# A two-layer transformer block on one core: the durations that its list scheduler assumes for TensorE and GpSimd are changed

## The chip, the cores and the metric

The kernel runs on one core of a Trainium2 chip, in one launch. A core has five instruction queues that run side by side and meet only at semaphores: TensorE (PE: matmuls and transposes), VectorE (DVE), ScalarE (ACT), GpSimd (POOL) and SyncE (SP), which here issues the DMAs. Each works through its instructions strictly in the order in which the program was written out for it. The metric is the device time of one execution in microseconds; the median of three is given. The profile comes from one more execution.

## The reference

A stack of two layers works on 256 tokens `x` and 256 context tokens `ctx`, both 1024 wide, in fp32. Each layer is a feed-forward block, a token mix (neighbourhood attention over the 256 tokens and the context with 8 heads of 64, beside a pooling mix over 4 groups of 128 channels), and a second feed-forward block. Every block is normed before and after, and modulated by nine vectors that come from a condition through a 1024 x 9216 matrix per layer.

```python
def sandwich_ffn(x, w_gate_up, w_down, g_pre, g_post, shift, scale, gate):
    h = modulate(rms_norm(x, g_pre), shift, scale)
    return x + 0.5 * gate * rms_norm(swiglu(h, w_gate_up, w_down), g_post)

for l in range(DEPTH):
    ...
    x = sandwich_ffn(x, w_ffn_gate_up[l, 0], w_ffn_down[l, 0], g[0], g[1], mx[0], mx[1], mx[2])
    ctx = sandwich_ffn(ctx, w_ffn_gate_up[l, 0], w_ffn_down[l, 0], g[0], g[1], mc[0], mc[1], mc[2])
    hx = modulate(rms_norm(x, g[2]), mx[3], mx[4])
    hc = modulate(rms_norm(ctx, g[2]), mc[3], mc[4])
    out_x, out_c = token_mix(hx, hc, w_in[l], w_out[l], na_rpb[l], w_pool[l], pool_scale[l], not last)
    x = x + mx[5] * rms_norm(out_x, g[3])
    x = sandwich_ffn(x, w_ffn_gate_up[l, 1], w_ffn_down[l, 1], g[4], g[5], mx[6], mx[7], mx[8])
    if not last:
        ctx = ctx + mc[5] * rms_norm(out_c, g[3])
        ctx = sandwich_ffn(ctx, w_ffn_gate_up[l, 1], w_ffn_down[l, 1], g[4], g[5], mc[6], mc[7], mc[8])
return x
```

## The kernel before

**Arithmetic.** Every fp32 operand of a large matmul is split into a high part in the matmul format `fp32r` and a low part, the rest. A product is three matmuls (`mm3`: high by high, high by low, low by high). Splitting is an ACT copy into the high half and a DVE subtraction into the low half (`split`, and the same in `Stream.prep` for weights). A weight tile of 1024 columns so costs one ACT and one DVE instruction of 1024 elements per partition; the tiles are called `w_big`.

**Stages.** The program runs `ffn(0, 0)`, `token_mix(0)`, `ffn(0, 1)`, `ffn(1, 0)`, `token_mix(1)`, `ffn(1, 1)`. A feed-forward block walks over 22 groups of 128 hidden columns: gate (`pg`) and up (`pu`), 24 matmuls each, the SiLU product, then the down matmuls into `pd`. Its hidden columns go in parts (`F_GROUPS`), the down matmuls of each part adding to `y_big`. In `ffn(1, 0)` the gate and up matmuls of a group are replaced by seven quarter products (`gate_up_seven`, tiles `p_ps`), whose sums of weights GpSimd forms (`prep_seven`, tiles `s_wk`). `close` ends a block per token tile: squares on ACT, `power` on GpSimd (a sum and a power of -0.5, tiles `rs`), scaling, and the transposes that make the next block's input.

**Attention.** `token_mix` runs the eight heads as chains (`head`): scores `pS` and `pC` on PE, maxima on DVE, exponentials on ACT, normalising, transposes `pp`, splitting, and the products `po`. Between them stand blocks of 24 column matmuls for the keys (`pk`), queries (`pq`) and the pooling input (`pu`) of the next pair of heads. `pooled` forms the window sums on GpSimd (`dd`), and `roped` turns keys and queries with one product on GpSimd and the rest on DVE.

**Filler.** The modulation vectors that later blocks need are accumulated on DVE (`acc`, from `wm` tiles of the modulation matrix) and added up on GpSimd (`part`), spread over the feed-forward blocks by `fill`.

**What sets the order.** Nothing is issued while these functions run. Each call is recorded (`Recorder.record`) as an operation with a price (`Recorder.price`), its dependencies by overlap of what it reads and writes, and its place in the record (`rank`). `Recorder.order` then plays a list schedule: every engine has a clock; of all operations whose inputs are done, the one that can start earliest by these clocks is taken, a lower `rank` first where two tie, with small head starts (`haste`) for the ends of blocks and for heads, and a `margin` for a few. It also decides from these times when a buffer place comes free (16 places for `big`, 2 for raw weights, 10 for `wk`, 8 PSUM banks, 24 for small statistics), which tile gets which place, and in which order SP issues the DMAs. `Recorder.issue` writes the operations out in that order. The prices do nothing else: no value, size or dependency depends on them. All operations so carry the line of `issue`, L387, in the profile, and are told apart by their tiles.

Of the kernel before, what the change touches and what calls it, by code (L numbers as in the profile page):

```python
# [12 lines left out]
F32R = mybir.dt.float32r  # L13
# [171 lines left out]
class Recorder:  # L185
# [30 lines left out]
    @staticmethod  # L216
    def price(engine, method, outs, ins, kw):
        size = max(int(np.prod(v.shape[1:])) for v in outs + ins if isinstance(v, View)) if engine != "sync" else 0
        far = any(isinstance(v, View) and v.buf.tag == "ps" for v in ins)
        pointers = sum(1 for v in ins if isinstance(v, View) and int(np.prod(v.shape[1:])) == 1 and size > 1)  # L220
        if engine == "tensor":
            n = int(np.prod(outs[0].shape[1:]))
            if method == "transpose":
                return 0.107
            return 0.003 + n / 2400.0 if ins[0].dtype == F32R else 0.19
        if engine == "scalar":
            extra = 0.093 * (min(pointers, 1) + (1 if "accum_out" in kw else 0))
            return (0.052 if far else 0.094) + size / 1200.0 + extra
        if engine == "vector":
            rate = 0.52 if method in ("tensor_scalar", "tensor_copy") and not far else 1.042  # L230
            return 0.068 + rate * size / 1000.0 + 0.061 * min(pointers, 2)
        if engine == "gpsimd":
            if method == "memset":
                return 0.03 + size / 1200.0
            if kw.get("op") == ALU.pow:
                return 0.464
            return 0.155 + 2.09 * size / 1000.0
        return 0.45

    def record(self, engine, method, args, kw):  # L240
# [1255 lines left out]
```

## Time and profile before

| | us |
|---|---|
| median of 3 executions | 1657.24 |
| their lowest and highest | 1656.57, 1659.04 |
| the profiled execution | 1658.03 |
| its span, first to last instruction | 1656.0 |
| mean granted TensorE clock | 0.996 of full |

The span is what the views of the profile divide; the other 2.0 us of the profiled execution lie around it. PE is TensorE's matmuls, PEld its weight loads beside them. A matmul's busy time reaches until its result is out, so successive matmuls overlap in the record. "Idle before" is the time that an engine stood still ahead of an instruction, with the engine or transfer that released it. The windows view gives busy times in stretches of the span; the chain is the work that ended last, followed back from the end. Busy times in tenths over 40 equal slices of the span show the parts: the first slice is the start, slices 11 to 14 hold the attention of layer 0, and 33 to 36 that of layer 1:

```
PE   6999999999999899999999999999999999899998
DVE  7985766546689779867776488677788778875554
ACT  7522322225566663222222264534444567774442
POOL 1022011101131311110211036363463122210000
```

### The profile page before, as it was taken

The page shows a single profiled execution, that of the slowest core. Times are in us where ns is not written, and L with a number is a line of the kernel's source. Part 1 is how long each engine was busy: PE and PEld are TensorE (multiplying, and loading weights), DVE is VectorE, ACT ScalarE, POOL GpSimd, SP SyncE. Part 2 cuts the span into 40 slices and gives each one's busy share as a digit, 9 for nine tenths or more (in the row PEclk, how much of TensorE's full clock was granted, in tenths as well). Part 3 has the DMA queues.
Part 4 walks back from the last instruction along what each step waited for, and adds up shares of the span by engine and source line. Part 5 has one row for each costly group of instructions (what it writes and reads, how often), then busy time and mean ns, then how long its engine had stood idle before and what let it go on. Part 6 is the DMA issues. An engine that isn't in the chain of part 4 may idle for free.

```text
span 1656.0 us, 23501 instructions
## 1 busy us (share of the span) xinstructions
PE 1613.0 (97%) x9074; PEld 1390.3 (84%) x9074; DVE 1212.7 (73%) x1662; ACT 736.6 (44%) x1292; POOL 356.9 (22%) x348
## 2 busy tenths in 40 slices
PE   6999999999999899999999999999999999899998
PEld 4988888888878689888888879999989888778997
DVE  7985766546689779867776488677788778875554
ACT  7522322225566663222222264534444567774442
POOL 1022011101131311110211036363463122210000
PEclk9999999999999999999999999999999999999999
DMA  9466556532221436666698412233233421355551
GB/s 376 185 230 243 209 194 225 175 118 83 86 78 65 157 108 223 235 204 230 211 351 300 159 52 96 83 103 127 77 116 114 144 90 70 132 200 199 196 200 55
DMA packets 98958, 269.09 MB, mean 162 GB/s; under 512 B 9424, under 2 KB 39328, under 8 KB 87072
## 3 DMA queue, kind: packets, MB, share of 16 engines
q1 hardware_dynamic: 98848, 267.60, 45.5%
q8 instruction: 71, 1.16, 0.3%
q14 instruction: 39, 0.32, 0.1%
HBM read 251.80 MB, written 1.09 MB: 153 GB/s over the span
## 4 chain that ended last, share of the span: by engine, by line
PE 84%; DVE 6%; ACT 5%; POOL 2%; issue 2%; DMA 1%; SPq 0%; POOLq 0%; DVEq 0%; ACTq 0%
PE pd_ps L387 26%; PE pu_ps L387 19%; PE pg_ps L387 19%; PE p_ps L387 11%; PE pv_ps L387 2%; ACT n_wk L387 2%; PE pk_ps L387 2%; POOL rs_st L387 2%; DVE w_big L387 1%; PE pq_ps L387 1%; DMA w_big<-in_wmod_dram 1%; PE pt_ps L387 1%; ACT sx_wk L387 1%; PE po_ps L387 1%; ACT w_big L387 1%
## 5 line engine op out<-in xcount | busy, mean ns | idle before, releaser
L387 DVE TENSOR_TENSOR w_big<-raw_raw,w_big 128x1024 fp32r<-128x1024 f32 x293 | 369.8, 1277 | 122.5 <-ACT w_big L387 122.2
L387 PE MATMUL pd_ps<-w_big,g_big 128*128 128x512 f32 x1848 | 430.7, 393 | 0.0
L387 PEld LDWEIGHTS pd_ps<-w_big,g_big 128*128 128x128 f32 x1848 | 345.7, 188 | 77.7 <-ACT grows L387 0.2
L387 ACT ACTIVATE w_big<-raw_raw 128x1024 fp32r<-128x1024 f32 x293 | 302.8, 1054 | 228.9 <-DMA raw_raw<-in_wgu_dram 94.6
L387 PE MATMUL pu_ps<-h_big,w_big 128*128 128x512 f32 (+1 forms) x1944 | 366.4, 341 | 0.0
L387 PEld LDWEIGHTS pu_ps<-h_big,w_big 128*128 128x128 f32 x1944 | 303.7, 188 | 42.5
L387 PE MATMUL pg_ps<-h_big,w_big 128*128 128x512 f32 (+1 forms) x1752 | 330.3, 342 | 1.4 <-ACT h_big L387 1.4
L387 PEld LDWEIGHTS pg_ps<-h_big,w_big 128*128 128x128 f32 x1752 | 275.6, 189 | 41.3 <-ACT h_big L387 1.8
L387 DVE SCALAR_TENSOR_TENSOR acc_wk<-wm_wk,csil,acc_wk 128x1024 f32<-128x1024 f32 x196 | 244.2, 1285 | 81.5 <-DMA wm_wk<-in_wmod_dram 81.2
L387 POOL TENSOR_TENSOR part_wk<-part_wk 128x512 f32<-128x512 f32 (+2 forms) x84 | 87.7, 1045 | 496.1 <-DMA part_wk<-acc_wk 418.5
L387 ACT ACTIVATE g_big<-tt_wk 128x512 fp32r<-128x512 f32 (+1 forms) x84 | 49.2, 586 | 275.6 <-DVE tt_wk L387 258.4
L387 POOL TENSOR_SCALAR rs_st<-sq_st 128x1 f32<-128x1 f32 x24 | 7.5, 312 | 448.8 <-ACT n_wk L387 448.7
L387 POOL TENSOR_TENSOR s_wk<-raw_raw 128x512 f32<-128x512 f32 x38 | 64.1, 1695 | 126.3 <-DMA raw_raw<-in_wgu_dram 120.5
L387 PE MATMUL p_ps<-h_big,w_big 128*128 128x256 f32 x684 | 86.8, 281 | 0.0
L387 PEld LDWEIGHTS p_ps<-h_big,w_big 128*128 128x128 f32 x684 | 83.5, 189 | 0.3
L387 PE MATMUL p_ps<-ht_big,w_big 128*128 128x256 f32 x684 | 82.9, 279 | 0.0
L387 PEld LDWEIGHTS p_ps<-ht_big,w_big 128*128 128x128 f32 x684 | 81.2, 189 | 0.0
L387 DVE TENSOR_TENSOR g_big<-tt_wk,g_big 128x512 fp32r<-128x512 f32 (+1 forms) x84 | 57.8, 688 | 29.3 <-ACT g_big L387 29.2
L387 PE MATMUL pd_ps<-w_big,mix_big 128*128 128x512 f32 x288 | 71.6, 397 | 0.5 <-DVE mix_big L387 0.5
L387 DVE TENSOR_TENSOR w_big<-s_wk,w_big 128x1024 fp32r<-128x1024 f32 x38 | 59.0, 1554 | 15.2 <-ACT w_big L387 15.2
L387 ACT ACTIVATE tt_wk<-pg_ps 128x512 f32<-128x512 f32 (+1 forms) x67 | 35.7, 533 | 75.9 <-PE pg_ps L387 65.8
L387 DVE TENSOR_TENSOR y_big<-y_big,pd_ps 128x512 f32<-128x512 f32 x72 | 48.4, 685 | 27.0 <-PE pd_ps L387 27.0
(157 smaller groups left out, 1771.7 us busy)
## 6 DMA issues: line engine op xcount, KB each, us to landing
raw_raw<-in_wgu_dram SPq DMA_DIRECT2D x84, 1024.0 KB, 4.9
wm_wk<-in_wmod_dram SPq DMA_DIRECT2D x128, 512.0 KB, 6.8
raw_raw<-in_wdn_dram SPq DMA_DIRECT2D x44, 1024.0 KB, 5.2
part_wk<-acc_wk SPq DMA_DIRECT2D x224, 64.0 KB, 2.4
raw_raw<-in_wkq_dram SPq DMA_DIRECT2D x8, 1024.0 KB, 4.8
raw_raw<-in_wout_dram SPq DMA_DIRECT2D x8, 1024.0 KB, 5.0
w_big<-in_wmod_dram SPq DMA_DIRECT2D x7, 1024.0 KB, 16.0
gb_wk<-grow SPq DMA_DIRECT2D x10, 512.0 KB, 6.9
```

Source lines behind the costliest of these rows:

```text
L387: getattr(getattr(nc, op.engine), op.method)(*[self.real(a) for a in op.args], **{k: self.real(a) for k, a in op.kw.items()})
```

## The change

Four lines of `Recorder.price` change, with five figures: the fixed part and the rate of an `fp32r` matmul, the transpose, GpSimd's power, and the rate of GpSimd's other elementwise operations. `n` is the number of output columns, `size` the elements per partition, and prices are in microseconds. The other engines' prices, the lags between engines, the assumed DMA speeds and all parameters of the schedule stay.

```diff
         if engine == "tensor":
             n = int(np.prod(outs[0].shape[1:]))
             if method == "transpose":
-                return 0.107
-            return 0.003 + n / 2400.0 if ins[0].dtype == F32R else 0.19
+                return 0.109
+            return 0.005 + n / 2265.0 if ins[0].dtype == F32R else 0.19
         if engine == "scalar":
...
             if method == "memset":
                 return 0.03 + size / 1200.0
             if kw.get("op") == ALU.pow:
-                return 0.464
-            return 0.155 + 2.09 * size / 1000.0
+                return 0.56
+            return 0.155 + 2.5 * size / 1000.0
         return 0.45
```

## Prediction

> **What bounds the kernel now.** I read the page's shares first, then the chain that ended last, then the span cut into stages, because a mean over stages hides where an order of operations can matter.
>
> ```profile
> span 1656.0 us, 23501 instructions
> PE 1613.0 (97%) x9074; PEld 1390.3 (84%) x9074; DVE 1212.7 (73%) x1662; ACT 736.6 (44%) x1292; POOL 356.9 (22%) x348
> PE 84%; DVE 6%; ACT 5%; POOL 2%; issue 2%; DMA 1%; SPq 0%; POOLq 0%; DVEq 0%; ACTq 0%
> ```
>
> TensorE is busy nearly throughout and holds 84% of the chain. The other 16% is all that a new order could touch, and some of it is fixed at the two ends. The stages, from the windows view (columns: stretch, its length, busy time and instructions of PE, PEld, DVE, ACT and POOL, granted clock, DMA share, GB/s):
>
> ```profile
> 0.00:37.50 37.50, 23.17 (x153) 16.44 (x153) 26.43 (x44) 27.77 (x48) 4.25 (x18) 1.00 0.94 371
> 612.00:697.00 85.00, 85.00 (x492) 74.56 (x492) 75.87 (x79) 28.09 (x38) 14.53 (x12) 1.00 0.60 217
> 1049.00:1300.00 251.00, 251.00 (x1834) 237.45 (x1834) 199.49 (x216) 108.75 (x141) 108.25 (x60) 1.00 0.32 110
> 447.60:569.00 121.40, 113.16 (x608) 93.69 (x607) 103.22 (x251) 81.94 (x207) 37.05 (x38) 0.99 0.28 94
> 1362.00:1447.00 85.00, 78.72 (x500) 69.03 (x499) 74.44 (x188) 61.36 (x148) 24.07 (x29) 1.00 0.31 112
> 1447.00:1489.00 42.00, 38.89 (x185) 31.80 (x185) 30.66 (x42) 29.60 (x53) 5.88 (x8) 0.96 0.54 198
> ```
>
> The first row is the start: DMA engines 94% busy, no order on TensorE shortens that. The next two are feed-forward stages, and PE is busy for their whole length. Only the last three, the attention parts of the two layers and the turn to the last feed-forward, leave PE idle.
>
> Busy time of pipelined matmuls is generous, so the durations are better taken from long unbroken runs of the chain in order of time (start, length, what):
>
> ```profile
> 264.87 44.22 PE pd_ps L387 x192
> 1234.35 59.13 PE p_ps L387 x504
> 456.65 0.87 PE pp_ps L387 x8
> ```
>
> A 512-wide matmul takes 44.22/192 = 0.2303 us, a 256-wide one 59.13/504 = 0.1173, a transpose 0.87/8 = 0.109. In layer 0's attention (447.6 to 569) the code issues 32 pS, 12 py, 72 k, 72 q and 96 u matmuls of 512, 32 pC and 144 po of 256, and 96 transposes, 556 together; the other 52 of the 608 are pd of 512. That is 336 x 0.2303 + 176 x 0.1173 + 96 x 0.109 = 108.5 us of 121.4: **12.9 us idle**. Layer 1 (1362 to 1447): 32 pS and 72 k of 512, 72 q, 96 u, 96 po and 12 py of 256, 64 transposes, and 56 pd by the remainder: 160 x 0.2303 + 276 x 0.1173 + 64 x 0.109 = 76.2 of 85: **8.8 us idle**. With the 42.00 - 38.89 = 3.1 us of the turn, some 25 us are within reach.
>
> **The change part by part.** No instruction is added or removed, no transfer, buffer or wait: the five edited figures feed only the list that decides, per engine and for SP's DMA queue, which ready operation goes next. I weigh each figure against the trace.
>
> TensorE: a 512-wide matmul goes from 0.003 + 512/2400 = 0.2163 to 0.005 + 512/2265 = 0.2310 (trace 0.2303), a 256-wide one from 0.1097 to 0.1180 (0.1173), a transpose from 0.107 to 0.109 (0.109). So the old list had TensorE 6% too quick, the new one is right to 1%.
>
> By the Trainium skill, TensorE: Matmul & The Clock Gate, section Back-to-back issue gap, an isolated warm matmul takes N/2.4 + 2.5 ns, 216 ns at 512: nearly the old figure, and by it the change would spoil a right price. The same section says a stream has another spacing, 131 ns; the trace has 230 ns over 192 in a row, so neither figure holds here.
>
> GpSimd, from the groups of instructions (count, busy us, mean ns, idle before) and one stretch of the timeline:
>
> ```profile
> L387 POOL TENSOR_TENSOR s_wk<-raw_raw 128x512 f32<-128x512 f32 x38 | 64.1, 1695 | 126.3 <-DMA raw_raw<-in_wgu_dram 120.5 <-DVE c_wk L387 5.8
> L387 POOL TENSOR_TENSOR part_wk<-part_wk 128x256 f32<-128x256 f32 x28 | 22.5, 803 | 2.2
> 394.95 0.56 POOL L387 TENSOR_TENSOR rs_st<-rs_st,nhalf 128x1 f32<-128x1 f32 x1
> ```
>
> A 512-wide add goes from 1.225 to 1.435 (trace 1.695), a 256-wide one from 0.690 to 0.795 (0.803), the power from 0.464 to 0.56 (0.56). All move toward the chip; the wide one stops short. In the stage with most POOL work (1049 to 1300) POOL is busy 108.25 of 251, so these figures alone I put at 0: its idle time hides them. Without that cover a 512-wide add that is late by 1.695 - 1.435 = 0.26 us, twice in a row before a split, would cost 0.5 us a time.
>
> **Feed-forward stages: 0.** Nothing there is faster than PE without a gap. It could only be lost, if weights come late: DVE's spare is 85.00 - 75.87 = 9.1 us per 85 in the fullest stretch. That cover is what the cost of 0 stands on. Filler for the modulation vectors moved forward can use it up, but only as far as the ten places of its buffers reach.
>
> **Attention: a gain.** Here the lists interleave head chains (scores, maxima, exponentials, transposes, products) with blocks of 24 column matmuls. Wherever the old list thought a block of 24 over, it was 24 x (0.2303 - 0.2163) = 0.336 us too early (256-wide: 24 x 0.0076 = 0.182), so an evacuation stood at the head of ACT's or DVE's queue before its data were there, with other ready work behind it. The waits view names such places (us in total, times, longest); the first two rows are of 447 to 560, the others of 1366 to 1490:
>
> ```profile
> ACT mix_big L387 <- PE po_ps L387: 5.4, 5, 1.6
> ACT pT_big L387 <- PE pp_ps L387: 3.8, 6, 1.2
> ACT mix_big L387 <- PE po_ps L387: 4.6, 4, 1.9
> ACT g_big L387 <- PE pt_ps L387: 4.5, 2, 2.7
> ACT mix_big L387 <- PE py_ps L387: 3.1, 1, 3.1
> ```
>
> They are 21.4 us over 18 waits. Layer 0 has 10 blocks of 512 (k 3, q 3, u 4): 3.4 us of misplacement. Layer 1 has 3 of 512 and 7 of 256: 1.0 + 1.3 = 2.3. The upper bound of the gain is thus 5.7 us, the lower one nothing. I take the share in which DVE has no slack to swallow it, 103.22/121.4 = 0.85 and 74.44/85 = 0.88 from the windows: 0.85 x 3.4 + 0.88 x 2.3 = 4.9 us. What is late next are DVE's own operations, which the list prices as before.
>
> **Sum.** The profiled execution took 1658.0 us, 1656.0 of span and 2.0 around it: 1658.0 - 4.9 = 1653.1. It lies 0.8 above the median of the three runs (1657.2), so on that scale the forecast is **1652**. A measurement of this kernel tells about 0.2%, 3.3 us, from no change.
>
> **The rivals.** *No difference* (1657): the waits that cost PE time in attention end with DVE, not with PE, and then a truer TensorE price moves nothing that is last. The timeline around PE's longest gap speaks for it:
>
> ```profile
> 532.11 5.72 PE L387 MATMUL pu_ps<-h_big,w_big 128*128 128x512 f32 x24
> 535.65 2.19 DVE L387 TENSOR_TENSOR w_big<-raw_raw,w_big 128x1024 fp32r<-128x1024 f32 x1
> 537.76 1.38 DVE L387 TENSOR_TENSOR rp_wk<-rp_wk 128x256 f32<-128x256 f32 x1
> 539.06 1.74 DVE L387 TENSOR_TENSOR w_big<-raw_raw,w_big 128x1024 fp32r<-128x1024 f32 x1
> 540.83 1.71 DVE L387 TENSOR_TENSOR qa_wk<-rp_wk,qa_wk 64x256 fp32r<-64x256 f32 x2
> 541.81 3.17 PE L387 MATMUL pS_ps<-kb_big,qa_wk 128*128 128x512 f32 x8 [3.86 <-DVE qa_wk L387]
> ```
>
> PE ended its block and stood 3.86 us because DVE put two weight splits between the rope and the query tile. That the list comes out almost the same is part of this case: 4.9 us that shrink below 3.3 land in it.
>
> *Slower, by weight splits in front of head chains.* With TensorE 6.8% longer the list sees 6.8% more room on DVE per block, and fills it with the next weights, ready early. On the chip that room isn't there:
>
> ```profile
> L387 DVE TENSOR_TENSOR w_big<-raw_raw,w_big 128x1024 fp32r<-128x1024 f32 x14 | 20.3, 1449 | 0.7 <-ACT w_big L387 0.5
> ```
>
> In 447.6 to 560 such a split takes 1.449 us, where the list has 0.068 + 1.042 x 1.024 = 1.135. Place: the stretch above and its counterparts. Price: one more tile pair ahead of a chain is 2 x 1.449 = 2.9 us; one pair in each layer gives +5.8, so 1663, two in each +11.6, so 1669. It decides from the point where DVE reaches the query tile later than PE ends its block, and at 541.81 that is already so. Against it: the splits have to be done anyway, and the sixteen places for weights limit how early.
>
> The Trainium skill, SBUF — State Buffer, section Who interferes with whom, says that a DVE operation with two SBUF inputs and a GpSimd one that reads SBUF exclude each other for a whole instruction. The splits of 2.19 and 1.74 us agree. By that rule no fixed GpSimd price is right beside such splits, which speaks for this rival.
>
> *Slower, since the true price is the old one.* If matmuls in the attention parts ran at the old figure, the new list would misplace blocks by about as much the other way: +4.9, so 1662. The 192 in a row at 0.2303 all but exclude it.
>
> **How the numbers follow.** Faster by the forecast's mechanism 0.43, no difference 0.27, slower by splits 0.28, slower by price 0.02. The lists are greedy, so a small shift early can reorder much behind it, hence no case is above a half. The range: below, the whole 12.9 us idle of layer 0's attention gained, which takes in the 5.7 of the bound, 1657 - 13 = 1644, set to 1643 for the tenths; above, two pairs in each layer, 1669. Both signs hold much; the likeliest case's own range is 1651 to 1654.
>
> **What would show it.** Right: after the change the waits of ACT for po, pp and pt in attention are shorter, those stretches end sooner by about 3 and 2 us, and PE is busy throughout in the feed-forward stages. Wrong: PE's wait for the query tile grows, or more splits stand between 447 and 569 than now (the slower rival), or PE waits for w_big in a feed-forward stage, which would break the cost of 0, or the gain comes at the start or the end, which no step explains.

## The result and the profile after

The changed kernel takes 1694.12 us (median of 5 runs, 1692.20 to 1696.96) against 1657.24 of the kernel before: a ratio of 1.0218, 95% interval 1.0207 to 1.0230. It is **37 us slower**, where 1652 was forecast and 1669 was the upper end of the range. From the page of the changed kernel, the span, the shares, the chain by engine and the chain by line:

```profile
span 1692.9 us, 23490 instructions
PE 1625.2 (96%) x9074; PEld 1394.4 (82%) x9074; DVE 1212.7 (72%) x1662; ACT 733.3 (43%) x1292; POOL 358.3 (21%) x348
PE 62%; DVE 13%; DMA 10%; ACT 5%; issue 4%; SPq 4%; POOL 2%; DVEq 0%; POOLq 0%; ACTq 0%
PE pd_ps L387 18%; PE pu_ps L387 13%; PE pg_ps L387 12%; PE p_ps L387 11%; DMA wm_wk<-in_wmod_dram 6%; DVE acc_wk L387 4%; SPq L387 4%; DMA raw_raw<-in_wgu_dram 3%; DVE w_big L387 3%; ACT n_wk L387 2%; POOL rs_st L387 2%; PE pv_ps L387 2%; PE pk_ps L387 2%; PE pq_ps L387 1%; PE pt_ps L387 1%
```

The busy time of every engine is the same to about 1%: only an order changed. But the chain has left PE: 84% of it were PE's, now 62%, and `wm` transfers, `acc` sums and SP's issuing have come in. Those are the filler that accumulates the modulation vectors. Before, SP's issuing had 0% of the chain and all transfers together 1%.

To see where the time went, I cut both spans at the first matmul of a kind in PE's timeline: the first `pv` of each layer, the first `pg` after attention, the first `p_ps`, the first `pd` of the last block, and the end of the last matmul. The stretches overlap a little at their seams, as the kernels interleave there. Each column is one profiled execution.

| stretch, us | before | after | difference |
|---|---|---|---|
| start and feed-forward (0, 0) | 411.8 | 413.7 | +1.9 |
| attention of layer 0 | 191.8 | 196.5 | +4.7 |
| feed-forward (0, 1) | 414.0 | 436.1 | **+22.1** |
| feed-forward (1, 0) | 311.1 | 312.0 | +1.0 |
| attention of layer 1 and the turn to the last block | 180.0 | 187.6 | +7.6 |
| from the first down matmul of (1, 1) | 140.1 | 139.8 | -0.3 |

Most of the loss lies in a feed-forward block that PE had filled almost without a gap. The windows view (columns as in the prediction) of the same stretch, first the kernel before, then the changed one:

```profile
860.00:920.00 60.00, 60.00 (x263) 48.73 (x263) 42.72 (x46) 15.11 (x19) 5.06 (x6) 1.00 0.80 281
```

```profile
860.00:920.00 60.00, 51.72 (x226) 41.89 (x224) 47.16 (x49) 13.38 (x15) 10.93 (x9) 0.95 0.86 303
```

PE stands still for 8.3 of 60 us, while DVE is not full either: 47 of 60. (The granted clock in these rows fell too, from 1.00 to 0.95.) So it isn't an engine without time, but a queue in the wrong order. The waits view of the changed kernel, PE alone, names it (total, times, longest):

```profile
PE pr_ps L387 <- DVE col L387: 15.2, 2, 9.9
PE pt_ps L387 <- DVE n_wk L387: 15.1, 10, 8.7
PE pt_ps L387 <- ACT n_wk L387: 5.3, 4, 1.9
```

The first row was not there before; the other two were 12.1 and 0.8. `pr` is the tiny transpose that turns a finished gate vector (`col`) into rows, in `finish_mod`; PE has its hundreds of gate and up matmuls behind it. In PE's timeline of the kernel before, the vector's last sum `pm` and its `pr` stand 20 + 16 = 36 matmuls apart:

```profile
781.17 0.28 PE L387 MATMUL pm_ps<-sel,part_wk 128*128 128x8 f32 x2
781.31 4.86 PE L387 MATMUL pu_ps<-h_big,w_big 128*128 128x512 f32 x20
786.00 3.86 PE L387 MATMUL pg_ps<-h_big,w_big 128*128 128x512 f32 x16
789.70 0.27 PE L387 MATMUL pr_ps<-ident,col 128*16 128x128 f32 x1
```

DVE had the vector ready 2.4 us ahead of that `pr`, at 787.11 + 0.17:

```profile
787.11 0.17 DVE L387 TENSOR_TENSOR col<-col,colt 128x16 f32<-128x16 f32 x1
```

In the changed kernel 22 + 8 = 30 matmuls stand between them:

```profile
789.37 0.28 PE L387 MATMUL pm_ps<-sel,part_wk 128*128 128x8 f32 x2
789.51 5.33 PE L387 MATMUL pu_ps<-h_big,w_big 128*128 128x512 f32 x22
794.68 2.00 PE L387 MATMUL pg_ps<-h_big,w_big 128*128 128x512 f32 x8
802.02 0.37 PE L387 MATMUL pr_ps<-ident,col 128*16 128x128 f32 x1 [5.34 <-DVE col L387]
```

Six matmuls are only 1.4 us, and the wait is 5.34. The rest is DVE being late. Its timeline in the changed kernel has `col` behind eight filler sums and two weight splits (two operations of 0.70 us are left out):

```profile
788.45 8.47 DVE L387 SCALAR_TENSOR_TENSOR acc_wk<-wm_wk,csil,acc_wk 128x1024 f32<-128x1024 f32 x7
...
797.41 1.29 DVE L387 SCALAR_TENSOR_TENSOR acc_wk<-wm_wk,csil,acc_wk 128x1024 f32<-128x1024 f32 x1
...
799.21 2.37 DVE L387 TENSOR_TENSOR w_big<-raw_raw,w_big 128x1024 fp32r<-128x1024 f32 x2
801.48 0.18 DVE L387 TENSOR_TENSOR col<-pm_ps,colt 128x16 f32<-128x16 f32 x1
```

At the second place DVE stands idle ahead of `col`, waiting for a `wm` tile, and PE waits 9.88 us:

```profile
911.30 1.28 DVE L387 SCALAR_TENSOR_TENSOR acc_wk<-wm_wk,csil,acc_wk 128x1024 f32<-128x1024 f32 x1 [4.12 <-DMA wm_wk<-in_wmod_dram]
```

The distance in matmuls doesn't explain this place: between `pm` and `pr` PE's timeline has 33 of them before and 40 after. Before, `col` was ready 1.7 us ahead of `pr`:

```profile
892.69 0.17 DVE L387 TENSOR_TENSOR col<-col,colt 128x8 f32<-128x8 f32 x1
894.54 0.27 PE L387 MATMUL pr_ps<-ident,col 128*8 128x128 f32 x1
```

Behind the wait the matmuls are slower too. The windows view has a granted clock of 0.50 there, and PE's timeline eight matmuls in 3.76 us, 0.47 us each where 0.23 is usual:

```profile
921.60:927.60 6.00, 6.00 (x15) 4.76 (x16) 3.39 (x3) 1.36 (x3) 0.00 (x0) 0.50 1.02 419
921.63 3.76 PE L387 MATMUL pu_ps<-h_big,w_big 128*128 128x512 f32 x8
```

With a like stretch behind the first place that makes, by my estimate from such rows, some 4 us. So of the block's 22.1 us 15.2 are the two waits and about 4 the slower matmuls behind them.

Why is the filler late? SP's queue, in the timeline of the kernel before, shows one thing that the list has wrong. The list prices every issue at 0.45 us. A vector's fold sends 16 small transfers `part<-acc`, and they take 10.18 us:

```profile
663.08 10.18 SPq L387 DMA_DIRECT2D part_wk<-acc_wk  x16
696.38 0.33 SPq L387 DMA_DIRECT2D raw_raw<-in_wgu_dram  x1
```

That is 0.636 us each, 0.186 more than priced, and what stands behind them in SP's queue, weights and `wm` tiles, can go out that much later than planned. The block has 128 of them: 128 x 0.186 = 24 us. (Its 34 loads of 1 MB are priced 0.07 to 0.12 too dear, which gives some 3 us back.) The old list had a second error over the same block that hid this one: some 1440 matmuls of 512 priced 0.0140 us short and 288 of 256 priced 0.0076 short make 22 us by which PE, too, was later than planned. **Two errors of nearly one size held each other up**; the change took one of them away. That is theory D below, reached after two others; a table behind the experiments sets the list's own times against the traces.

### The profile page after: what moved, and what is told of

It reads as the page before. It is cut to its first block, busy times and chain, and to the rows that moved or that the text cites. A ratio compares the mean times of both kernels' runs of the same rounds, so it can differ in the third digit from the quotient of the medians.

```text
span 1692.9 us, 23490 instructions
## 1 busy us (share of the span) xinstructions
PE 1625.2 (96%) x9074; PEld 1394.4 (82%) x9074; DVE 1212.7 (72%) x1662; ACT 733.3 (43%) x1292; POOL 358.3 (21%) x348
## 4 chain that ended last, share of the span: by engine, by line
PE 62%; DVE 13%; DMA 10%; ACT 5%; issue 4%; SPq 4%; POOL 2%; DVEq 0%; POOLq 0%; ACTq 0%
PE pd_ps L387 18%; PE pu_ps L387 13%; PE pg_ps L387 12%; PE p_ps L387 11%; DMA wm_wk<-in_wmod_dram 6%; DVE acc_wk L387 4%; SPq L387 4%; DMA raw_raw<-in_wgu_dram 3%; DVE w_big L387 3%; ACT n_wk L387 2%; POOL rs_st L387 2%; PE pv_ps L387 2%; PE pk_ps L387 2%; PE pq_ps L387 1%; PE pt_ps L387 1%
## 5 line engine op out<-in xcount | busy, mean ns | idle before, releaser
L387 PE MATMUL pg_ps<-h_big,w_big 128*128 128x512 f32 (+1 forms) x1752 | 334.0, 345 | 0.1
L387 DVE TENSOR_TENSOR g_big<-tt_wk,g_big 128x512 fp32r<-128x512 f32 (+1 forms) x84 | 54.2, 645 | 34.7 <-ACT g_big L387 34.6
L387 DVE TENSOR_TENSOR w_big<-s_wk,w_big 128x1024 fp32r<-128x1024 f32 x38 | 57.9, 1525 | 15.6 <-ACT w_big L387 15.5
L387 PEld LDWEIGHTS pd_ps<-w_big,mix_big 128*128 128x128 f32 x288 | 53.5, 192 | 16.3 <-DVE w_big L387 2.1
```

Of the source, the lines that this page charges most:

```text
L387: getattr(getattr(nc, op.engine), op.method)(*[self.real(a) for a in op.args], **{k: self.real(a) for k, a in op.kw.items()})
```

## The experiments

All times are medians beside runs of the kernel before on the same chip. The stretches are the table's, as differences from the kernel before: attention 0, the block (0, 1), attention 1 with the turn. They come from one profiled execution of each kernel, which can lie some us from its median (e12 4.5 above, e5 3.9, e7 and e9 3.3, e10 3.7 below). Kernels whose attention has the very same order (e9 and e12, for one) differ there by up to 1.8 us, so smaller differences say nothing.

**Which of the prices.** Two kernels with half of the change each, and two with another margin ahead of `pm` and `pr`:

```diff
-MARGIN = 6.0
+MARGIN = 16.0    # e3, on the changed kernel
+MARGIN = 3.0     # e4, on the kernel before
```

> The three TensorE figures new, the two GpSimd figures old. Theory A (the TensorE price is the cause: with it the list puts the modulation vectors' last steps, the sums pm and the gate-row transposes pr, too few matmuls behind the loads and sums they depend on): most of the loss is here, 1680 to 1695 us, and PE waits for DVE's col at pr for about 15 us. Rival B (the GpSimd prices): within 5 us of 1657, no wait at pr. Rival C (any shift of the list costs, wherever it comes from): slower too, but the loss is spread and not at pr.

Measured 1687.86 us, 1.0174 (1.0157 to 1.0191). Attention 0 +7.5, the block +16.6 with 12.2 us of waits at `pr`, attention 1 +2.1. The TensorE figures carry the loss, as theory A has it.

> The two GpSimd figures new, the three TensorE figures old. Theory A: 1652 to 1662 us, no wait at pr. Rival B: 1680 to 1695. Rival C: 1665 to 1690, at other places than after the change.

Measured 1663.70 us, 1.0025 (1.0014 to 1.0036): +1.6, +0.8, +2.5, no wait at `pr`. It is a little beyond the band of theory A, and far from rival B's. The GpSimd figures alone, which the prediction had put at 0, cost some 4 us, mostly in attention.

> All five new figures, and the margin that the list keeps ahead of the pm sums and pr transposes raised from 6 to 16 us, so that PE has more matmuls between a vector's last DMA and its transpose. Theory A: the 15.2 us of PE's waits at pr go, and 1672 to 1682 us are left, the rest being lost in the attention parts. Rival C: the time stays within 5 us of 1694, with PE waiting elsewhere in the second feed-forward block.

Measured 1692.65 us, 1.0199 (1.0184 to 1.0214). **Theory A falls here.** The waits at `pr` are gone, yet the block is still 22.0 us longer. The waits view of this kernel has the loss at other matmuls:

```profile
PE pd_ps L387 <- DVE col L387: 9.6, 2, 5.6
```

Rival C had asked for just this. The down matmuls too wait for `col`, and DVE, ahead of the `col` of the first of these waits, for a late `wm` tile:

```profile
845.54 1.31 DVE L387 SCALAR_TENSOR_TENSOR acc_wk<-wm_wk,csil,acc_wk 128x1024 f32<-128x1024 f32 x1 [9.25 <-DMA wm_wk<-in_wmod_dram]
```

PE's waits in the block are 15.6 us together, against 3.2 before; most of the rest is that its granted clock is 0.50 in four pieces of the block, 20.5 us long together, and was 1.00 throughout before. So `pr` is where the lateness showed, not what made it.

> All five old figures, and the same margin cut from 6 to 3 us: if theory A is right, the old price hid a lack of margin that a smaller margin brings out, with PE waiting at pr or pm and 1662 to 1675 us. Rival C: a time anywhere from 1650 to 1690 without waits at pr. If the old list has enough room of its own (only the feed-forward's loads are late in the new one): 1655 to 1659.

Measured 1665.84 us, 1.0038 (1.0023 to 1.0053): the block +8.5 with one wait of 4.9 us at `pr`, attention unmoved (0.0 and 0.0). The wait is at the second place, so the old list had less than 3 us to spare there; its trace has 1.7.

**Theory D: SP's issue price.** The edit in `record`:

```diff
-            op.cost = 0.45
+            op.cost = 0.636 if outs and outs[0].buf.name == "part" else 0.45
```

> All five new figures, and a sixth: SP's issue of one of the small transfers that fold a modulation vector (part<-acc, 16 in a row) priced at 0.636 us, as the trace has it (16 in 10.18 us), in place of 0.45. Theory D (the list is late in the second feed-forward block because SP takes 3.0 us longer per vector than it assumes, 128 issues x 0.186 = 24 us there, so raw weights and wm tiles queue behind; the old TensorE price, 6% short, hid it by 26 us of plan): that block's loss of 22 us goes to under 5, and 1670 to 1680 us are left, with no wait at pr. Rival C (any other order is as bad): 1685 or more, or the block still 15 us longer than before the change.

Measured 1674.15 us, 1.0100 (1.0083 to 1.0117). The block falls from +22.1 to +5.4, with a single wait of 1.79 us left at `pr`; attention stays at +5.7 and +7.7. The theory holds for the block; its band of under 5 us and its "no wait" were missed by a little.

> All five old figures, and the same issue price of 0.636 us alone. Theory D: the second feed-forward block was held by PE anyway, so it stays within 3 us, and the total at 1650 to 1662. Rival C: a changed order costs by itself, 1662 to 1690.

Measured 1658.40 us, 1.0002 (0.9992 to 1.0011), the block +0.2. With the old TensorE figures the true issue price neither helps nor hurts. Rival C had asked for 1662 or more here and 1685 or more in e5, or 15 us left in the block: for the block it is out.

**How near the edge the old list stood.**

```diff
-            return 0.003 + n / 2400.0 if ins[0].dtype == F32R else 0.19
+            return 0.003 + n / 2390.0 if ins[0].dtype == F32R else 0.19    # e7; e8 has 2560.0
```

> All five old figures but the matmul rate, n/2390 for n/2400: a 512-wide matmul 0.0009 us dearer, a sixteenth of the change's step. It measures how much the attention parts move by themselves when the list is nudged. Theory (attention loses in the change because any reordering of that stage moves it by several us, either way): attention of both layers together moves by 2 to 10 us, either sign. Rival (the loss there grows with the price): under 1 us, total 1656 to 1660.

Measured 1660.66 us, 1.0017 (1.0006 to 1.0028). Attention moved by +1.2 and -0.5, less than the theory of this run asked for. But the block took +5.2, at this row of the waits view:

```profile
PE pr_ps L387 <- DVE col L387: 3.4, 2, 3.2
```

It is at the second place again. A matmul 0.4% dearer in the list brings the first 3 us of waiting.

> All five old figures but the matmul rate, n/2560: TensorE priced still 6% shorter, the step of the change in the other direction. Theory D: the second feed-forward block stays held by PE, within 3 us. If the loss in attention grows with the price, attention gains 3 to 10 us and the total is 1648 to 1655; if any reordering moves it, 1650 to 1675.

Measured 1659.70 us, 1.0007 (0.9998 to 1.0017): attention -0.9 and +2.9, the block -0.4. A TensorE price that is still further off does no harm to the block, and the loss in attention doesn't simply grow with the price.

**Theory E: the partners' prices in attention.** Heads are made of short DVE operations and of splits on 64 partitions. The groups of the kernel before give them longer means than the list's 0.07 and 0.335:

```profile
L387 DVE TENSOR_TENSOR sm_st<-sm_st 128x2 f32<-128x2 f32 x32 | 6.9, 216 | 5.5 <-ACT sx_wk L387 5.3
L387 DVE TENSOR_TENSOR qa_wk<-rp_wk,qa_wk 64x256 fp32r<-64x256 f32 x16 | 9.3, 581 | 1.9 <-ACT qa_wk L387 1.5
```

I took such figures for DVE's true prices, and that was a misreading. DVE's rows overlap, so the length of a row isn't what the operation costs the queue. Four rows of a run without gaps, in the attention of layer 0 before, show it:

```profile
486.04 0.17 DVE L387 TENSOR_SCALAR sc_st<-sc_st 128x2 f32<-128x2 f32 x1
486.11 0.69 DVE L387 TENSOR_TENSOR ds_wk<-dd_wk,ds_wk 128x512 fp32r<-128x512 f32 x1
486.71 1.22 DVE L387 TENSOR_TENSOR w_big<-raw_raw,w_big 128x1024 fp32r<-128x1024 f32 x1
487.85 0.69 DVE L387 TENSOR_TENSOR pT_big<-pp_ps,pT_big 128x512 fp32r<-128x512 f32 x1
```

The next operation starts 0.07, 0.60 and 1.14 us later. The old list has 0.070, 0.602 and 1.135, and adds a lag of 0.127 where an operation needs the result of the one before. So the old DVE prices fit such a run; the chip is slower than they say in places, such as the splits of 2.19 and 1.74 us in the prediction's timeline. Of ScalarE's figures in the edit the one for two pointers is borne out: four `yg` operations in a row take 1.49 us at 408.52, where the old list has 0.252 each. On the whole, what the edit tries, beside SP's of e5, is longer prices for the partners, not truer ones:

```diff
         if engine == "scalar":
             extra = 0.093 * (min(pointers, 1) + (1 if "accum_out" in kw else 0))
+            extra += 0.11 if pointers > 1 or outs[0].shape[0] == 64 else 0.0
             return (0.052 if far else 0.094) + size / 1200.0 + extra
         if engine == "vector":
             rate = 0.52 if method in ("tensor_scalar", "tensor_copy") and not far else 1.042
-            return 0.068 + rate * size / 1000.0 + 0.061 * min(pointers, 2)
+            if size <= 16:
+                return 0.18
+            two = method in ("tensor_sub", "tensor_add", "tensor_mul") and not far
+            half = outs[0].shape[0] == 64
+            return 0.068 + rate * size / 1000.0 + 0.061 * min(pointers, 2) + (0.1 if two or half else 0.0)
```

> All five new figures, SP's fold transfers at 0.636 us, and VectorE's and ScalarE's figures set nearer to the trace too: 0.18 us for DVE operations of up to 16 elements (they had 0.07, the trace 0.17 to 0.20 back to back), 0.1 us more for DVE with both inputs in SBUF or 64 partitions, 0.11 more for ACT with two pointers or 64 partitions. Theory E (the list goes wrong where one engine's price is true and those of its partners are short; set them all and it comes right): attention's loss of 13 us in both layers goes to under 5, the second feed-forward block within 5 us of before, total 1652 to 1664. Rival F (the attention parts move with any reordering, and truth does not help): attention still 8 us or more longer, total 1668 to 1685.

Measured **1658.95 us**, 1.0005 (0.9995 to 1.0014): the whole loss is gone. Attention +1.7 and -2.0, the block +0.6. At the first place PE's timeline has 22 + 14 = 36 matmuls between the same `pm` and `pr` again, as before the change, and no wait:

```profile
783.31 0.28 PE L392 MATMUL pm_ps<-sel,part_wk 128*128 128x8 f32 x2
783.45 5.28 PE L392 MATMUL pu_ps<-h_big,w_big 128*128 128x512 f32 x22
788.57 3.44 PE L392 MATMUL pg_ps<-h_big,w_big 128*128 128x512 f32 x14
791.84 0.27 PE L392 MATMUL pr_ps<-ident,col 128*16 128x128 f32 x1
```

> All five new figures, and the prices of VectorE, ScalarE and SP's issues multiplied by 1.068, the step that the 512-wide matmul made, so that the ratios are the old ones though no price is nearer to the chip for it. Theory E': only the ratios matter; attention and the second feed-forward block within 4 us of before, total 1653 to 1664. Rival F: attention still 8 us or more longer, total 1668 to 1690.

Measured 1677.64 us, 1.0118 (1.0096 to 1.0140): attention -1.1 and +5.6, the block +11.3 with 9.1 us at `pr`. Old ratios bring back about half. That fits neither expectation: the total is in rival F's band, attention is not. The list's lags, its transfer times and the margin were not scaled; whether that is what is missing wasn't tried.

> The edits of the run before last for VectorE, ScalarE and SP on the old TensorE and GpSimd figures. If longer prices for TensorE's partners are what helps, attention gains 2 to 8 us and the total is 1648 to 1656; by rival F 1655 to 1675.

Measured 1668.37 us, 1.0062 (1.0046 to 1.0078): attention +1.9 and +6.8, the block +0.7. This is in rival F's band: longer partner prices don't help by themselves. In attention either half of the edit alone loses, 12.3 us in the changed kernel and 8.7 here, and both together don't.

> As the run with all prices set, but SP's issue back at 0.45: all five new figures and the VectorE and ScalarE figures nearer to the trace. It parts the two causes. If SP's price is what makes the second feed-forward block late and VectorE's and ScalarE's what loses in attention: attention within 4 us of before, the block 10 to 24 us longer with PE waiting at pr, total 1668 to 1682. If the VectorE figures alone slow the filler enough in the list: the block within 5 us of before, total 1655 to 1664.

Measured 1669.91 us, 1.0068 (1.0052 to 1.0085): attention -0.1 and -2.7, the block +14.5 and (1, 0) behind it +5.3. The waits view:

```profile
PE pr_ps L392 <- DVE col L392: 13.3, 3, 11.8
```

SP's price mends most of the block and leaves attention (e5), VectorE's and ScalarE's mend attention and leave most of the block (e12), both together mend both (e9).

**The plan against the trace.** `Recorder.order` gives a time for every operation, and it can be computed from each kernel's code. The table compares these times with the trace, both counted from the first gate matmul of the block: how late SP's issues and PE's large matmuls are between 270 and 290 us (medians), ahead of the second place, and how long PE then waits at that `pr`. It has every kernel with the margin of 6.

| kernel | SP late, us | PE late, us | SP more than PE | wait at the second `pr` |
|---|---|---|---|---|
| e8 | 30.7 | 33.8 | -3.1 | 0 |
| e6 | 17.3 | 18.3 | -1.0 | 0 |
| e11 | 18.3 | 18.5 | -0.2 | 0 |
| e2 | 25.4 | 19.2 | 6.2 | 0 |
| before | 24.7 | 18.4 | 6.3 | 0 |
| e9 | 8.6 | 1.3 | 7.3 | 0.28 |
| e5 | 12.5 | 4.1 | 8.4 | 1.79 |
| e7 | 27.8 | 17.7 | 10.1 | 3.21 |
| e10 | 16.0 | 1.1 | 14.9 | 9.09 |
| after | 26.0 | 9.6 | 16.4 | 9.88 |
| e12 | 19.7 | 2.3 | 17.4 | 11.76 |
| e1 | 21.1 | 3.1 | 18.0 | 11.53 |

Before the change SP was about as late as after it; PE was late too, and met no wait. PE waits where SP is more than some 7 us later against the plan than PE itself, as theory D has it. (In the changed kernel PE's 9.6 us hold its wait at the first place.)

**Rival F stays open for attention.** e9 and e12 have one and the same order there, and it is the only one of eight new orders that isn't longer than before; e7's is 0.7 us longer and e8's 2.0, near the spread, the others 4 to 13. Since e9's DVE figures aren't truer ones, these runs can't tell the merit of longer partner prices from luck with one order.

## Why the prediction was wrong

- **"No instruction is added or removed"** and **"the new one is right to 1%"** (of TensorE's price) held: 504 matmuls of 256 columns in a row take 59.38 us in the changed kernel, 0.1178 each, where its list has 0.1180. The e9 kernel has the change's five figures in it and loses nothing, so the figures alone don't make the loss.
- **"Feed-forward stages: 0" is the step that failed**, by 23 of the 37 us in two blocks. Its argument was that PE is busy without a gap and DVE has 9.1 us spare per 85. A gapless stage shows that the order was good enough, not by how much. The measure would have been the time from when `col` is ready until PE reaches `pr`: the kernel before had 2.4 and 1.7 us left at the two places, and there PE waits 15.2 us after the change. I looked at DVE's share, where the late thing was SP's queue, of which I took no row at all.
- **The margin behind the cover was mis-seen.** The text named the filler and bounded it by ten buffer places. It hardly ran further ahead: counted in matmuls from the block's start, none of the block's eight groups of 16 fold transfers starts more than 20 earlier than before, and three start later. PE's small operations that end it came in front of their data.
- **"Attention: a gain" of 4.9 us failed in sign**: +4.7 and +7.6. The waits on which the gain was counted did shrink, from 21.4 to 10.5 us (the same rows in 447 to 560 and in 1396 to 1520 of the changed kernel; with the rows that came in beside them, all of ACT's waits for PE there went from 32.1 to 25.7):

```profile
ACT mix_big L387 <- PE po_ps L387: 3.4, 5, 1.2
ACT pT_big L387 <- PE pp_ps L387: 0.4, 1, 0.4
ACT mix_big L387 <- PE po_ps L387: 2.1, 2, 1.5
ACT g_big L387 <- PE pt_ps L387: 0.5, 1, 0.5
ACT mix_big L387 <- PE py_ps L387: 4.1, 1, 4.1
```

  So this sign of being right came true without the time: these waits of ACT weren't what the stages' length hung on. What made the 12 us instead stays open; the runs show that they aren't there in e9's and e12's order.
- **GpSimd's figures at 0**: alone they measured some 4 us (e2).
- **The rival of weight splits in front of head chains** had the sign and the size in attention, but not its mechanism. Its mark came true in the prediction's window, with 17 splits in place of 15 and the same busy time:

```profile
L387 DVE TENSOR_TENSOR w_big<-raw_raw,w_big 128x1024 fp32r<-128x1024 f32 x17 | 21.3, 1257 | 1.7 <-ACT w_big L387 1.6
```

  Counted between the cuts of the table, though, there are 26 splits in the attention of layer 0 and 43 in that of layer 1, before and after, and PE's waits for the query tile, which should have grown, fell from the first row to the second:

```profile
PE pS_ps L387 <- DVE qa_wk L387: 5.7, 3, 3.9
PE pS_ps L387 <- DVE qa_wk L387: 3.2, 3, 1.8
```

  Its price of a split, 1.449 us against the list's 1.135, also takes the overlap of DVE's rows for cost.
- **The rival that the old price is the true one** is out: 504 matmuls in a row take 59.38 us after and 59.13 before, and e9 is as fast with the new price.
- **The range** reached up to 1669 by two misplaced pairs per layer. It counted losses in attention alone, since the feed-forward blocks had been set to 0 with no upper end.

What stays open: what loses the 12 us in attention, and which of the VectorE and ScalarE figures of e9, if any for more than luck, brings them back; and the first 1.9 us of the span, where PE's waits at `pt` grew from 8.7 to 11.1 us. No kernel tried here beats the kernel before; the best are level with it.

## What to carry to other kernels

A list scheduler's prices work together: correcting one engine's to the measured value can take away the slack that another queue's error was living on, so compare the list's own times with the trace for all engines and queues, the issuing of small transfers included, before one price is set. Take a price from the distance between the starts of operations in a run without gaps, not from the length of their rows. When a tuned order runs without a gap, ask how long each small late-fed operation in the bound engine's queue stands behind its data; that time, not busy shares, is the room a change has. And when a wait is removed and the time stays, it was the place where a delay showed: look for what is late upstream.

## What the runs showed of the hardware

SP mostly needs 0.33 to 0.38 us to issue one 1 MB load of weights but 0.636 us, in a row, for one 64 KB transfer that spreads a 128-column slice of 128 partitions onto 16 partitions (16 in 10.18 us in the kernel before and again in e9). The smaller transfer is the dearer one to issue. The Trainium skill, DMA: Bandwidth & Descriptors, section "Anatomy of one DMA — SWDGE (gpsimd) path", gives about 50 ns for a sequencer's dispatch on GpSimd's path; SP's issues here aren't on that path, and both rows are some seven to thirteen times that figure.

Behind PE's waits of 5.34 and 9.88 us the granted clock is 0.50 for a while, and matmuls of 0.23 us take 0.47; the kernel before had a clock of 1.00 over that block. A wait so cost more than its own length.

A DVE operation on two elements has a row 0.17 us long, but an independent one follows 0.07 us after its start.
